# A hybrid decoder trunk: the order of projections, state-space quarters and attentions, and the value products of two heads side by side

## The chip, the cores and the metric

The kernel runs on one core of a Trainium2 chip. The metric is the device time of one launch in microseconds (us), as the median of several runs. Everything is in 32-bit floats; the large products use pairs of rounded numbers (a high and a low part, type fp32r) so that three fast products stand for one exact one.

## The reference

The input is one sequence of 512 tokens with 1024 features. Two layers follow. Layer 0 mixes tokens in two ways side by side: half of the features go through a diagonal state-space model (32 groups of 16 channels with 64 complex states), the other half through "stick-breaking" attention (8 heads of 64). Layer 1 is a convolution module. After each mixer come a residual, a layer norm, a feed-forward layer with squared ReLU, and again a residual and a layer norm. The part that matters here:

```python
h = x @ mix_w_in[i] + mix_b_in[i]
u, q, k, v = jnp.split(h, [512, 1024, 1536], axis=-1)
s5_out = s5_mixer(u, ...)             # states, gelu, then a gated linear unit (glu)
# attention, per head, strictly causal:
z = einsum(q, k) * scale
log_beta = log_sigmoid(z)
log_keep = where(strict, log_sigmoid(-z), 0.0)
after = cumsum(log_keep, reverse=True) - log_keep
weights = where(strict, exp(log_beta + after), 0.0)
out = einsum(weights, v)
mix = concatenate([s5_out, sb_out]) @ mix_w_out[i] + mix_b_out[i]
```

## The kernel before

Features lie on the 128 partitions and the 512 tokens along the free dimension. Before the change's place the input is transposed and the first projection `u` is made. Then layer 0's mixer runs as a list of steps, `ORDER`, for four quarters of the features (two heads of attention, or a quarter of the state-space groups, each):

- `q0` to `q3` (function `qkv`): three projections, each 24 products of 512 columns through `in_proj` and `gemm` (L206). The result stays in a PSUM bank of the tag `mm` (three banks) until it is copied into `qh`, `ql`, `kh`, `kl` (one buffer each) or `v` (two buffers).
- `s0` to `s3` (`s5_states`): VectorE (DVE) prepares Gx and Cx, TensorE (PE) makes gp, tp, vR and vI, and DVE runs a chain of products and two scans that ends in Sx. Gx, Cx, Tx and Sx have one buffer each, so a quarter's step waits for the outputs of the quarter before.
- `y0` to `y3` (`s5_outputs`): yp, twelve products of 128 columns from Tx, Cx, Sx, then U is updated on DVE.
- `a0` to `a3` (`attention`), described below.
- `gelu`: GELU of all four quarters, with a Tanh on ScalarE (ACT) and a round trip through device memory on the sync engine's (SP's) queue, back into `yf` (tag `wt`, three buffers).
- `glu`: 96 products into `mm` banks, with a Sigmoid for each of four gates.

After the list, `accum` multiplies the state-space half with half of the output matrix (`acmo`, 96 products), and the attention half follows in `tail_norm_lead`.

An attention step has two heads, 0 and 1, which lie on partitions 0 to 63 and 64 to 127. Each head has three groups of score blocks: A (key block 0 against all 512 queries), B (key blocks 1 and 3, 384 and 128 columns), C (key block 2, 256 columns). The string `ATT` lists the order of the groups' steps. `s` is `scores`: products of 64 rows into a bank of the tag `z` (four banks, shared with gp, tp, vR, vI, yp and vt), then Abs, Exp, Ln on ACT, a DVE step, a mask on GpSimd (POOL), and the split into high and low parts; these (`sh`, `sl`) have one buffer for each letter, which both heads share. `w` is `weigh`: products with `tri` and `negs` (constants for the sums over later keys) into the same bank, then Exp into a `wt` buffer (three), a mask on POOL, and, before the change, the value products into the bank `av`, 64 output columns for each head (L685).

The instructions of each engine run in an order that is fixed when the kernel is built: by the order in which the code emits them as far as their inputs and buffers are ready in the builder's plan. The buffers and banks of one tag are handed out in the order of the code. The weights come through `Weights`: raw blocks by DMA on SP's queue, then a high part on ACT (`whi`) and a low part on DVE (`wlo`), two units ahead. `Act` puts a table load on ACT before a function of another set, and ties it behind all functions of the set before: Exp and Ln are one set, Tanh and Sigmoid another. `add_manual_dep` with `NOSYNC` fixes an order on one engine and makes nothing wait.

Of the kernel before, what the change touches and what calls it, by code (L numbers as in the profile page):

```python
# [13 lines left out]
ALU = mybir.AluOpType  # L14
PSUM = bass.MemoryType.PSUM

P = 128
T = 512
# [23 lines left out]
AHEAD = (5, 4)  # L42
FJ = 3
BEFORE = (1, 3, 1, 2)
ATT = "sB0 sC0 wB0 sA0 wC0 sB1 sC1 wB1 sA1 wC1 wA1 wA0"
MIX_BUFS = (3, 4, 1, 4, 3)
WARM = 24
QK_BUFS = (1, 1)
ORDER = "q0 s0 a0 q1 y0 s1 a1 q2 y1 s2 a2 q3 y2 s3 y3 gelu a3 glu".split()


class Weights:
# [56 lines left out]
def units_of(name, w, k0, nk, cols, width):  # L109

    ncol = 1024 // nk
    out = []
    for c in cols:
        base = c // width * width
        src = w[k0 * P : (k0 + nk) * P, base : base + width].rearrange("(k p) n -> p k n", p=P)
        out.append(((name, k0, base), src, nk, ncol, c - base, width))
    return out
# [5 lines left out]
NOSYNC = mybir.DependencyInfo(mybir.DependencyClass.NoSync, mybir.DependencyReason.DATA)  # L123
# [23 lines left out]
def kernel(ctx: ExitStack, tc: tile.TileContext, a: dict, out: bass.AP):  # L147
    nc = tc.nc
    act = Act(tc)
    V, S, G, PE = nc.vector, nc.scalar, nc.gpsimd, nc.tensor  # L150
# [7 lines left out]
    def page(name, dt=F32R):  # L158
        return pgp.tile([P, T], dt, tag="pg", name=name, bufs=24)
# [35 lines left out]
    def split(hi, lo, src):  # L195
        i0 = S.copy(hi, src).ins  # L196
        i1 = V.tensor_sub(lo, src, hi.bitcast(F32)).ins  # L197
        return i0.name, i1.name
# [19 lines left out]
    units = units_of("u", w_in, 0, 8, range(0, 512, 128), 128)  # L218
    for o in ORDER:
        if o[0] == "q":  # L220
# [8 lines left out]
    def psum(tag, name, bufs):  # L229
        return mps.tile([P, T], F32, tag=tag, name=name, bufs=bufs)  # L230
# [4 lines left out]
    def zz(name):  # L235
        return psum("z", name, MIX_BUFS[1])
# [41 lines left out]
    for n in vecs:  # L278
# [3 lines left out]
        while done < m:  # L282
            half, at = divmod(r0 + done, P)
            c = min(m - done, P - at)
# [19 lines left out]
    for j in range(KT):  # L304
        ps = (mm if j % 2 else s5ps)(f"xT{j}")
        for b in range(4):
            ins = PE.transpose(ps[:, b * P : (b + 1) * P], xin[j][:, b, :], ident).ins
# [12 lines left out]
        if j == 2:  # L320
            parp = zz("parp")
            ins = PE.transpose(parp[:, :96], nat, ident[:96, :96]).ins
# [26 lines left out]
    def stt(o, x, s, y, op0, op1):  # L349
        V.scalar_tensor_tensor(o, x, s, y, op0=op0, op1=op1)  # L350
        return o

    def exps(x):
        xc = ts(small(), x, -87.0, 88.0, ALU.max, ALU.min)
        k = ts(small(), xc, LOG2E, MAGIC, ALU.mult, ALU.add)
        ts(k, k, MAGIC, None, ALU.subtract, ALU.bypass)
        r = stt(small(), k, -LN2HI, xc, ALU.mult, ALU.add)
        stt(r, k, -LN2LO, r, ALU.mult, ALU.add)
        s = ts(small(), r, 1.0 / math.factorial(8), None, ALU.mult, ALU.bypass)
        for n in range(7, 0, -1):  # L360
            stt(s, s, 1.0 / math.factorial(n), r, ALU.add, ALU.mult)
        ki = ts(small(16, I32), k, 127.0, 8388608.0, ALU.add, ALU.mult)
        p2 = ki.bitcast(F32)
        e = stt(small(), s, 1.0, p2, ALU.add, ALU.mult)
        m = tt(small(), s, p2, ALU.mult)
        em1 = stt(small(), p2, -1.0, m, ALU.add, ALU.add)
        return e, em1

    ts(LR, LR, -1e-4, None, ALU.min, ALU.bypass)
    dt, _ = exps(LDT)  # L370
# [50 lines left out]
    for k in (2, 3, 4):  # L421
        h = 1 if k < 4 else 2
# [202 lines left out]
    def attention(p, q_, k_, v_):  # L625
        vps = zz(f"vt{p}")
        for b in range(4):
            PE.transpose(vps[:, b * P : (b + 1) * P], v_[:, b * P : (b + 1) * P], ident)
        vt = att.tile([P, 4, P], F32, tag="vt", name=f"vt{p}")
        S.copy(vt, vps.rearrange("p (b c) -> p b c", b=4))  # L630
        av = psum("av", f"av{p}", MIX_BUFS[2])

        groups = {}
        for h in range(2):
            groups[f"A{h}"] = ((h, 0, 0),)
            groups[f"B{h}"] = ((h, 1, 0), (h, 3, 384))
            groups[f"C{h}"] = ((h, 2, 0),)
        at = {(h, kb): (g, o) for g, bl in groups.items() for h, kb, o in bl}
        diag = {"A": slice(0, 1), "B": slice(0, 4, 3), "C": slice(0, 1)}
        zs, sps, summed = {}, {}, [0, 0]  # L640

        def mask(x, g):
            x = x.rearrange("p (b c) -> p b c", c=P)[:, diag[g[0]], :]
            G.affine_select(x, x, pattern=[[0, x.shape[1]], [1, P]], compare_op=ALU.is_gt, fill=0.0,
                            base=0, channel_multiplier=-1)

        def scores(g):
            z = zs[g] = zz(f"z{p}{g}")
            for h, kb, o in groups[g]:
                R = slice(64 * h, 64 * h + 64)  # L650
                for i, (u, v) in enumerate(((0, 0), (0, 1), (1, 0))):
                    ins = PE.matmul(z[:, o : o + T - P * kb], k_[u][R, P * kb : P * kb + P], q_[v][R, P * kb :],
                                    start=o == 0 and i == 0, stop=i == 2, skip_group_check=True).ins
                    if o or i:
                        tc.add_manual_dep(ins, opened, NOSYNC, reason="the bank's first product")
                    opened = ins.name
            n = H if g[0] == "C" else T
            z = z[:, :n]
            sp = att.tile([P, T], F32, tag="spt", name=f"sp{p}{g}", bufs=MIX_BUFS[3])[:, :n]
            act(sp, z, AF.Abs)  # L660
            act(sp, sp, AF.Exp, scale=-1.0)
            act(sp, sp, AF.Ln, bias=1.0)
            stt(sp, z, 0.0, sp, ALU.max, ALU.add)
            mask(sp, g)
            hi = att.tile([P, n], F32R, tag=f"sh{g[0]}", name=f"sh{p}{g}", bufs=1)
            lo = att.tile([P, n], F32R, tag=f"sl{g[0]}", name=f"sl{p}{g}", bufs=1)
            split(hi, lo, sp)
            sps[g] = (hi, lo)

        def weigh(g):  # L670
            for h, kb, o in groups[g]:
                for k2 in range(3, kb - 1, -1):
                    g2, o2 = at[h, k2]
                    n = T - P * k2
                    for i in range(2):
                        PE.matmul(zs[g][:, o + P * (k2 - kb) : o + P * (k2 - kb) + n], tri if k2 == kb else negs,
                                  sps[g2][i][:, o2 : o2 + n], start=False, stop=k2 == kb and i == 1, skip_group_check=True)
            n = H if g[0] == "C" else T
            w_ = att.tile([P, T], F32, tag="wt", name=f"w{p}{g}", bufs=MIX_BUFS[4])[:, :n]
            act(w_, zs[g][:, :n], AF.Exp)  # L680
            mask(w_, g)
            for h, kb, o in groups[g]:
                R = slice(64 * h, 64 * h + 64)
                summed[h] += 1
                PE.matmul(av[R, P * kb :], vt[:, kb, R], w_[:, o : o + T - P * kb], start=summed[h] == 1,  # L685
                          stop=summed[h] == 4, skip_group_check=True)

        for x in ATT.split():
            (scores if x[0] == "s" else weigh)(x[1:])
        ch, cl = page(f"ch{p}"), page(f"cl{p}")  # L690
        split(ch, cl, av)
        cat[4 + p] = (ch, cl)
# [40 lines left out]
    hq = {}  # L733
    for o in ORDER:
        if o[0] == "q":
            hq[o[1]] = qkv(int(o[1]))
        elif o[0] == "a":
            attention(int(o[1]), *hq[o[1]])
        elif o[0] == "s":
            s5_states(int(o[1]))  # L740
        elif o[0] == "y":
            s5_outputs(int(o[1]))
        elif o == "gelu":
            gelu()
        else:
            glu()
# [210 lines left out]
    for n in ("ln1_g", "ln2_g", "conv_ln_g"):  # L957
        c = PV[:, vrow[n] : vrow[n] + a[n].shape[0] * KT]
# [148 lines left out]
    for bi, nb in enumerate(FFN_BLOCKS[1]):  # L1107
# [3 lines left out]
        if bi < len(FFN_BLOCKS[1]) - 1:  # L1111
            for f in range(2):
                pss = [nps(f"g{bi}{f}{b}") for b in range(4)]
                for k in range(0, nb, 2):
                    wh, wl = W.next()
                    for b in range(4):
                        for kk in range(2):
                            hh, hl = (t_[:, b * P : (b + 1) * P] for t_ in hs[k + kk])
                            for i, (u, v) in enumerate(((hh, wh), (hl, wh), (hh, wl))):
                                PE.matmul(pss[b], u, v[:, kk, :], start=k + kk == 0 and i == 0,  # L1120
                                          stop=k + kk == nb - 1 and i == 2)
# [68 lines left out]
```

## Time and profile before

| | us |
|---|---|
| median of 3 runs | 1278.25 (1272.75 to 1278.43) |
| the profiled execution | 1277.66, its span 1275.9 |
| PE busy | 1212.0 (95% of the span) |
| DVE busy | 778.6 (61%) |
| ACT busy | 564.8 (44%) |
| POOL busy | 109.5 (9%) |
| mean granted TensorE clock | 0.972 of full speed |

PE, DVE, ACT and POOL are the engines TensorE, VectorE, ScalarE and GpSimd; PEld is PE's loading of weights. A row of a timeline gives the start and the length of one or several merged instructions, the engine, the line of the code, what is written and what it is read from (buffer numbers and the head's number are left out: z1B is block B of attention 1, of either head), and in brackets the idle time just before and what ended it. The ends of PE's products are modelled, so prices are taken from start to start. A 32-bit float product that isn't fp32r shows as two records. The attentions' value products run from 83 to 98 us (attention 0), 128 to 145, 175 to 193, and 239 to 254.

### The profile page before, as it was taken

What the parts mean: (1) busy time and instruction counts of PE and PEld (TensorE: products, weight loads), DVE (VectorE), ACT (ScalarE), POOL (GpSimd) and SP (SyncE); (2) the same over time, 40 slices, a digit from 0 to 9 for tenths busy, and PEclk for the clock granted to TensorE, in tenths of its full rate; (3) what the DMA queues carried; (4) which work ended last, traced back from release to release, by engine and by line L of the source; (5) the groups of instructions that cost most, each with busy time, mean ns of one, the idle gap of its engine ahead of it and who ended that gap; (6) DMA issues with size and microseconds to landing.
All of it is one profiled execution on the core that took longest, in us unless ns stands there. A gap on an engine that the chain in (4) does not pass through costs nothing.

```text
span 1275.9 us, 16671 instructions
## 1 busy us (share of the span) xinstructions
PE 1212.0 (95%) x6559; PEld 1026.5 (80%) x6559; DVE 778.6 (61%) x1321; ACT 564.8 (44%) x1019; POOL 109.5 (9%) x145
## 2 busy tenths in 40 slices
PE   8799998799999999999999999789899999999997
PEld 7677766578988888888899888788898888888886
DVE  6967467357853443433448999999873343444436
ACT  5855364633541422422425675796463241322230
POOL 1011120103000000000031001114310000000000
PEclk9999888899999999999999999979999999999999
DMA  7511101234243233333302320003143232323211
GB/s 186 157 34 50 34 18 43 57 116 133 67 133 98 99 99 99 99 100 99 103 24 78 99 100 1 34 2 100 34 141 111 73 109 79 116 83 116 75 59 66
DMA packets 111662, 105.93 MB, mean 83 GB/s; under 512 B 9378, under 2 KB 99746, under 8 KB 111584
## 3 DMA queue, kind: packets, MB, share of 16 engines
q1 hardware_dynamic: 111424, 104.84, 26.1%
q8 instruction: 51, 0.84, 0.3%
q14 instruction: 27, 0.22, 0.1%
q10 hardware_dynamic: 160, 0.03, 0.0%
HBM read 100.66 MB, written 4.19 MB: 82 GB/s over the span
## 4 chain that ended last, share of the span: by engine, by line
PE 75%; DVE 15%; ACT 3%; issue 3%; DMA 2%; POOL 1%; SPq 1%; DVEq 0%; ACTq 0%; POOLq 0%
PE f L206 22%; PE g L1120 11%; PE acf L206 10%; PE fl L206 4%; PE h L1104 3%; PE tld L206 3%; DVE cz L350 2%; PE tlb L206 2%; PE cv L1019 2%; DVE cy L350 2%; PE acmo L206 2%; DVE wlo L90 2%; PE pl L206 1%; PE pv L206 1%; PE v L206 1%
## 5 line engine op out<-in xcount | busy, mean ns | idle before, releaser
L90 DVE TENSOR_TENSOR wlo<-raw,whi 128x1024 fp32r<-128x1024 f32 x176 | 220.6, 1257 | 250.4 <-ACT whi L89 236.9
L89 ACT CAST whi<-raw 128x1024 fp32r<-128x1024 f32 x176 | 183.9, 1049 | 414.2 <-PE f L206 111.4
L1120 PE MATMUL g<-whi,hh 128*128 128x512 f32 x208 | 81.5, 392 | 0.0
L1120 PE MATMUL g<-wlo,hh 128*128 128x512 f32 x208 | 81.5, 392 | 0.0
L1120 PE MATMUL g<-whi,hl 128*128 128x512 f32 x208 | 81.4, 391 | 0.0
L206 PE MATMUL f<-xdh,whi 128*128 128x512 f32 x208 | 80.9, 389 | 0.0
L206 PE MATMUL f<-xah,whi 128*128 128x512 f32 x208 | 80.9, 389 | 0.0
L206 PE MATMUL f<-xal,whi 128*128 128x512 f32 x208 | 80.9, 389 | 0.0
L206 PE MATMUL f<-xdh,wlo 128*128 128x512 f32 x208 | 80.9, 389 | 0.0
L206 PE MATMUL f<-xdl,whi 128*128 128x512 f32 x208 | 80.9, 389 | 0.0
L206 PE MATMUL f<-xah,wlo 128*128 128x512 f32 x208 | 80.9, 389 | 0.0
L206 PE MATMUL acf<-hl,whi 128*128 128x512 f32 x192 | 75.2, 392 | 0.0
L206 PE MATMUL acf<-hh,whi 128*128 128x512 f32 x192 | 74.9, 390 | 0.0
L206 PE MATMUL acf<-hh,wlo 128*128 128x512 f32 x192 | 74.7, 389 | 0.0
L196 ACT CAST hh<-fr 128x512 fp32r<-128x512 f32 x64 | 39.7, 621 | 71.4 <-DVE fr L346 71.4
L197 DVE TENSOR_TENSOR hl<-fr,hh 128x512 fp32r<-128x512 f32 x64 | 44.2, 692 | 37.3 <-ACT hh L196 37.2
L350 DVE SCALAR_TENSOR_TENSOR cy<-hp,wdw,cy 128x512 f32<-128x512 f32 (+1 forms) x91 | 60.9, 678 | 0.1
L350 DVE SCALAR_TENSOR_TENSOR cz<-hp,wdw,cz 128x512 f32<-128x512 f32 (+1 forms) x86 | 59.8, 699 | 0.0
L1019 PE MATMUL cv<-hph,dh 128*128 128x256 f32 (+1 forms) x113 | 39.9, 353 | 10.0 <-ACT hph L196 8.3
L346 DVE TENSOR_TENSOR fr<-fr 128x512 f32<-128x512 f32 x64 | 43.8, 685 | 5.4 <-ACT fr L135 5.4
L1120 PEld LDWEIGHTS g<-whi,hl 128*128 128x128 f32 x208 | 39.1, 188 | 8.6
L1120 PEld LDWEIGHTS g<-wlo,hh 128*128 128x128 f32 x208 | 39.1, 188 | 8.6
(684 smaller groups left out, 3202.2 us busy)
## 6 DMA issues: line engine op xcount, KB each, us to landing
raw<-in_ffn_w_dram SPq DMA_DIRECT2D x48, 1024.0 KB, 5.4
raw<-in_ffn_w_dram SPq DMA_DIRECT2D x32, 512.0 KB, 3.6
raw<-in_conv_w_pw_dram SPq DMA_DIRECT2D x12, 1024.0 KB, 5.4
raw<-in_mix_w_in_dram SPq DMA_DIRECT2D x16, 512.0 KB, 3.9
xin<-in_x_dram SPq DMA_DIRECT2D x8, 256.0 KB, 3.8
raw<-in_s_w_glu_dram SPq DMA_DIRECT2D x4, 512.0 KB
raw<-in_mix_w_out_dram SPq DMA_DIRECT2D x4, 512.0 KB
raw<-in_mix_w_out_dram SPq DMA_DIRECT2D x2, 1024.0 KB
```

The lines of the kernel that those rows point to most:

```text
L89: i0 = nc.scalar.copy(hi, raw).ins
L90: i1 = nc.vector.tensor_sub(lo, raw, hi.bitcast(F32)).ins
L196: i0 = S.copy(hi, src).ins
L197: i1 = V.tensor_sub(lo, src, hi.bitcast(F32)).ins
L206: ins = PE.matmul(ps[:, c0:c1], u[:, k, ksl], v[:, c0:c1], start=start and k == 0 and i == 0, stop=stop and k == n - 1 and i == 2).ins
L346: V.tensor_tensor(o, x, y, op=op)
L350: V.scalar_tensor_tensor(o, x, s, y, op0=op0, op1=op1)
L1019: PE.matmul(cps[j][:, c0:c1], u, v[:, t + c0 : t + c1], start=t == 0 and i == 0, stop=t == n - 1 and i == 2)
L1104: PE.matmul(ps, u, v, start=k == 0 and i == 0, stop=k == nk - 1 and i == 2)
L1120: PE.matmul(pss[b], u, v[:, kk, :], start=k + kk == 0 and i == 0, stop=k + kk == nb - 1 and i == 2)
```

## The change

`ORDER` puts each `y` behind its `s`, two quarters of the state-space model ahead of attention 0, `gelu` ahead of attention 2 and `glu` ahead of attention 3. The value products leave `weigh` and become a step of their own, `v`, in `ATT`: for each key block, head 0's product and head 1's one after the other, each tied behind the other head's mask. In `ATT` head 0's blocks are scored in the order C, A, B, and head 1's B directly behind head 0's B.

```diff
-ATT = "sB0 sC0 wB0 sA0 wC0 sB1 sC1 wB1 sA1 wC1 wA1 wA0"
+ATT = "sC0 sA0 sB0 sB1 wC0 wB0 sC1 wB1 vB sA1 wA0 wC1 vC wA1 vA"
...
-ORDER = "q0 s0 a0 q1 y0 s1 a1 q2 y1 s2 a2 q3 y2 s3 y3 gelu a3 glu".split()
+ORDER = "q0 s0 y0 s1 y1 a0 q1 s2 y2 a1 s3 y3 q2 gelu a2 q3 glu a3".split()
...
-            mask(w_, g)
-            for h, kb, o in groups[g]:
-                R = slice(64 * h, 64 * h + 64)
-                summed[h] += 1
-                PE.matmul(av[R, P * kb :], vt[:, kb, R], w_[:, o : o + T - P * kb], start=summed[h] == 1,
-                          stop=summed[h] == 4, skip_group_check=True)
+            ws_[g] = w_, mask(w_, g)
+
+        def values(c):
+
+            for (_, kb, o), _ in zip(groups[c + "0"], groups[c + "1"]):
+                for h in range(2):
+                    R = slice(64 * h, 64 * h + 64)
+                    summed[h] += 1
+                    ins = PE.matmul(av[R, P * kb :], vt[:, kb, R], ws_[f"{c}{h}"][0][:, o : o + T - P * kb],
+                                    start=summed[h] == 1, stop=summed[h] == 4, skip_group_check=True).ins
+                    tc.add_manual_dep(ins, ws_[f"{c}{1 - h}"][1], NOSYNC, reason="both heads together")
 
         for x in ATT.split():
-            (scores if x[0] == "s" else weigh)(x[1:])
+            {"s": scores, "w": weigh, "v": values}[x[0]](x[1:])
```

`mask` now returns the name of its instruction; nothing else changes.

More of the change, by code (lines that the diff above doesn't have):

```diff
@@ L639, in attention @@
         diag = {"A": slice(0, 1), "B": slice(0, 4, 3), "C": slice(0, 1)}
-        zs, sps, summed = {}, {}, [0, 0]
+        zs, sps, ws_, summed = {}, {}, {}, [0, 0]
         def mask(x, g):
             x = x.rearrange("p (b c) -> p b c", c=P)[:, diag[g[0]], :]
-            G.affine_select(x, x, pattern=[[0, x.shape[1]], [1, P]], compare_op=ALU.is_gt, fill=0.0,
-                            base=0, channel_multiplier=-1)
+            return G.affine_select(x, x, pattern=[[0, x.shape[1]], [1, P]], compare_op=ALU.is_gt, fill=0.0,
+                                   base=0, channel_multiplier=-1).ins.name
         def scores(g):
```

## The prediction

> **What bounds the kernel now.** I read the page's first two parts, then the busy time by stretch up to the end of the first output products, then the timelines of TensorE (PE), VectorE (DVE) and ScalarE (ACT) in the stretches that showed idle time. The page first:
>
> ```profile
> span 1275.9 us, 16671 instructions
> ...
> PE 1212.0 (95%) x6559; PEld 1026.5 (80%) x6559; DVE 778.6 (61%) x1321; ACT 564.8 (44%) x1019; POOL 109.5 (9%) x145
> ...
> PE   8799998799999999999999999789899999999997
> ...
> PEclk9999888899999999999999999979999999999999
> ```
> TensorE is the bound over the whole span, and its two weak places lie in the first quarter, which is where the change is. The stretches of that quarter (columns: width, busy time of PE, weight loads, DVE, ACT, POOL, then the granted TensorE clock):
>
> ```profile
> 64.00:98.40 34.40, 32.49 (x157) 23.09 (x152) 21.48 (x36) 19.23 (x39) 5.61 (x13) 0.95 0.11 32
> 98.40:145.60 47.20, 44.28 (x270) 33.35 (x269) 29.81 (x53) 22.36 (x45) 6.95 (x13) 0.93 0.12 34
> 145.60:193.00 47.40, 44.29 (x270) 33.59 (x269) 29.96 (x53) 24.36 (x46) 6.70 (x13) 0.93 0.11 34
> 193.00:232.00 39.00, 26.76 (x192) 23.18 (x191) 28.31 (x51) 19.94 (x35) 0.95 (x3) 0.73 0.26 72
> 232.00:272.00 40.00, 37.94 (x160) 27.32 (x160) 17.98 (x26) 21.43 (x34) 3.10 (x9) 0.96 0.15 49
> 272.00:292.00 20.00, 19.88 (x87) 16.12 (x87) 10.23 (x14) 4.41 (x5) 0.00 (x0) 1.00 0.36 122
> ```
> From 64 to 292 us (the last is where the first half of the output projection, `acmo`, ends) PE is busy 32.49 + 44.28 + 44.29 + 26.76 + 37.94 + 19.88 = 205.6 of 228 us: 22.4 idle. Where the clock is granted at c of full speed I count (1 - c) of the busy time as lost: 0.05 x 32.49 + 0.07 x 44.28 + 0.07 x 44.29 + 0.27 x 26.76 + 0.04 x 37.94 = 1.6 + 3.1 + 3.1 + 7.2 + 1.5 = 16.5. So 38.9 of the 228 us are lost, and 189.1 are work at full clock. Half of the loss, 12.2 + 7.2 = 19.4, lies in 193 to 232. What happens there:
>
> ```profile
> 208.87 0.49 PE L563 MATMUL yp<-U,Tx 128*128 128x128 f32 x2 [1.47 <-ACT Tx L528]
> 209.19 0.60 PE L628 MATMUL vt<-ident,v 128*128 128x128 f32 x4
> ...
> 221.66 0.68 PE L652 MATMUL z3B<-qh,kh 64*128 64x384 f32 x1 [1.21 <-DVE U L350]
> ...
> 229.40 0.48 PE L676 MATMUL z3B<-sh3B,negs 128*128 128x128 f32 x1 [5.89 <-ACT sh3B L196]
> ```
> ```profile
> 224.75 1.28 ACT L137 ACT_TABLE_LOAD   x1
> ```
> ```profile
> 224.00:228.00 4.00, 0.00 (x0) 0.00 (x0) 1.64 (x3) 3.97 (x8) 0.00 (x0) 0.50 0.62 157
> ```
> Attention 3 runs beside `s3`, `y3` and `gelu` and nothing else is left to fill PE: the projections are used up and `glu` waits for `gelu`. The head-1 block of z3B (221.66) waits until U has read yp3, because the four PSUM banks of the tag `z` are handed out in program order and yp3 (208.87) has one of them ahead of vt3 (209.19); then the Exp of the attention stands behind the last Tanh and a table load, and PE idles 5.89 us.
>
> **The change part by part.**
>
> *Value products as neighbours.* The count of instructions is the same. Each value product writes 64 output columns: head 0 on partitions 0 to 63, head 1 on 64 to 127. Price alone, from their starts:
>
> ```profile
> 83.40 1.08 PE L685 MATMUL av<-w0B,vt 128*64 128x384 f32 x4
> 84.31 0.59 PE L685 MATMUL av<-w0C,vt 128*64 128x256 f32 x2
> 84.84 0.38 PE L652 MATMUL z0C<-qh,kl 64*128 64x256 f32 x1
> ...
> 95.31 1.07 PE L685 MATMUL av<-w0A,vt 128*64 128x512 f32 x2
> 96.31 0.50 PE L206 MATMUL k<-x0h,whi 128*128 128x512 f32 x1
> ```
> B takes 84.31 - 83.40 = 0.91, C 84.84 - 84.31 = 0.53, A 96.31 - 95.31 = 1.00: 2.44 us a head, 4.88 an attention, 19.5 in four. Do two products on different output columns run together? The `tp` products (32 output columns each) show it:
>
> ```profile
> 205.26 1.72 PE L521 MATMUL tp<-Cx,Gx 128*32 128x128 f32 x62
> 206.91 0.49 PE L535 MATMUL vI<-U,gt 128*128 128x128 f32 x2
> ```
> ```profile
> L521 PE MATMUL tp<-Cx,Gx x256: 196/246/421, 59.3 to 206.7; 128*32 128x64 f32 x37, 128*32 128x128 f32 x36, 128*32 128x96 f32 x28, 128*32 128x32 f32 x27
> ```
> ```profile
> 64.40 1.16 PE L533 MATMUL vR<-U,gt 128*128 128x128 f32 x8
> 65.40 1.06 PE L535 MATMUL vI<-U,gt 128*128 128x128 f32 x8
> ```
> Eight records of 128 columns take 65.40 - 64.40 = 1.00 us, 0.125 each. A quarter's 64 records of `tp` average 80 columns, so alone they would take 64 x 0.125 x 80/128 = 5.0 us; they took 206.91 - 205.26 = 1.65. Four column groups run side by side at a third of the sum. Two groups then give at best half of 19.5 = 9.8 us; the other end is 0 (other instructions set between them). I take 8, nearer to the `tp` row, less a little for pairs that get separated.
>
> The Trainium skill ("TensorE: Matmul & The Clock Gate", "What overlaps and what doesn't") says that matmuls start and end strictly in program order. With two records per product (x4 rows for the two products of B) only head 0's second and head 1's first would overlap: 5/16 of B and a quarter of C and A would go, 1.3 us an attention, 5.4 in four, an estimate by that rule; the sum would come out 2.6 us later. The `tp` rows speak against it.
>
> *Score blocks.* Row groups (64 of 128 rows) already overlap between heads where blocks meet in the queue; before, that is A of head 0 with B of head 1:
>
> ```profile
> 68.15 0.39 PE L652 MATMUL z0A<-qh,kh 64*128 64x512 f32 x1
> 68.36 0.44 PE L652 MATMUL z0B<-qh,kh 64*128 64x384 f32 x1
> ```
> After, it is B with B. A and B of a head have 1,536 columns each, so the overlap is worth the same; and as yp keeps one of four banks in attentions 0 to 2, head 1's B comes late there. Between -1 and +1 us; I take 0. The first weighing now waits for the third block processed (B of head 0 comes after C and A), not the first: one Exp-Ln-mask round later, but the same four blocks are processed before PE goes on with head 1; covered by projection work, cost 0, and 1 to 2 us per attention if that cover is gone (the 6 us stall below holds it).
>
> *Order of quarters.* `y` moves directly behind its `s`, and `s0 y0 s1 y1` ahead of attention 0. Two sides. The loss: attention 0's banks come behind yp1 in program order. By the following rows, it is 14.5 us from the end of one quarter's yp (106.01 + 0.61 = 106.62) to the end of the next quarter's Sx (119.88 + 1.28 = 121.16), and the attention ends 23.7 us after Sx (143.78 + 1.07 = 144.85).
>
> ```profile
> 106.01 0.61 PE L565 MATMUL yp<-Sx,Cx 128*128 128x128 f32 x4
> ...
> 108.91 1.16 PE L533 MATMUL vR<-U,gt 128*128 128x128 f32 x8
> ```
> ```profile
> 74.06 1.28 DVE L346 TENSOR_TENSOR Sx<-m,n 128x508 f32<-128x508 f32 x2
> ...
> 119.88 1.28 DVE L346 TENSOR_TENSOR Sx<-m,n 128x508 f32<-128x508 f32 x2
> ```
> ```profile
> 143.78 1.07 PE L685 MATMUL av<-w1A,vt 128*64 128x512 f32 x2
> ```
> So: Sx0 ends at 75.3, yp0 (2.7 us) at 78, Sx1 at 93, attention 0 at about 117, against 98 before. But y0, s1, y1 are then done, which before stood only at 154. PE has until 117: the rest of s0, y0, s1 and y1 (12), q1 (three projections of 5.46, row below), a first one of q2, and attention 0 (17 by difference: 189.1 less nine projections of 5.46, less 96 products each for glu and acmo at 5.46/24, less about 27 for the quarters, over four), together about 51 of 53 us. The cover is thin: the projections are held by three `mm` banks, since qh and kh have one buffer, so k2 and v2 cannot start before attention 0 has read q0 and k0. I charge 3.5 us more than the 3.5 lost before in 64 to 98 (1.9 idle + 1.6 clock).
>
> ```profile
> 98.48 5.46 PE v L206 x24
> ```
> *Attentions 1 and 2.* s2 and y2 now stand before attention 1 and s3, y3, q2 before attention 2, with a next projection to fill. Each window holds as much as 98 to 145 (43 us of work, less 2 for the pairs), so each keeps that row's loss, 2.9 + 3.1 = 6.0 us: a short wait in the fixed order, and then half clock:
>
> ```profile
> 124.00:128.00 4.00, 2.57 (x16) 1.93 (x14) 3.09 (x7) 2.36 (x6) 1.95 (x3) 1.00 0.45 131
> 128.00:132.00 4.00, 3.78 (x10) 1.90 (x11) 2.51 (x6) 0.48 (x2) 1.02 (x3) 0.63 0.00 0
> 132.00:136.00 4.00, 4.00 (x14) 3.61 (x15) 1.99 (x4) 3.02 (x6) 0.00 (x0) 0.51 0.00 2
> ```
> *gelu before attention 2, glu before attention 3.* `Act` ties each table load behind all functions of the set before. So attention 2's Exps wait for the Tanh of quarter 3, hence for y3: the wait of 221 to 229 moves from attention 3 to 2, where q3 (16.4 us) can fill. Attention 3's Exps wait for glu's four sigmoids, hence for most of glu's 96 products (96/24 x 5.46 = 21.8 us), with one table load more, 1.28 us. Behind that, attention 3 has 21.8 us of acmo beside it. So the 19.4 us in 193 to 232 shrink to a window's usual 6.0. The DMAs that gelu issues on the sync engine's (SP's) queue wait for the same Tanh, and raw weights stand behind them:
>
> ```profile
> SPq L707 <- DVE g L350: 19.3, 2, 17.5
> ```
> In this row they wait 17.5 us and nothing urgent is behind; after, q3's or glu's raws can be. Bounds 0 and 17.5; I take 3, since raws are fetched two units ahead. yf0 to yf3 also go through the three `wt` buffers ahead of attention 2's weights: it needs those only some 5 us after its scores; 0.
>
> *The end.* acmo's last product comes 189.1 - 8 = 181 us of work after 64, plus losses: 7.0 in the first window, 6.0 each in three others, 3 for gelu's DMAs, 1.5 at the end of the stretch (gaps as in 252 to 272, half of 3.6) = 29.5. That is 64 + 210.6 = 274.6 against 292: 17.4 earlier. Later stages are the same; the weights of the first feed-forward layer need the memory of the attention pool, which is free at the end of attention 3. I find that at about 250, against 254 before, so nothing is lost there: 0, up to 5 if it ends late.
>
> The profiled execution took 1277.66 us (span 1275.9 and 1.8 around it), 0.6 under the median of 1278.25. 1277.66 - 17.4 is 1260; I forecast **1260 us**.
>
> **The rivals.**
> 1. *More of the loss goes* (PE is fed in every window). s and y chains no longer queue behind projections, so chain and fill run together: losses of 3 rather than 6 in three windows, none from DMAs, the full 9.8 for pairs: 17.4 + 9 + 3 + 1.8 = 31 earlier, 1246 us. For it: 189.1 us of work is all that PE has to do. Against: the fixed queue, and 43 of 47 us in 98 to 145 although q2 was there to fill.
> 2. *The idle time only moves.* Attention 2 gets the stretch that attention 3 had: q3 and k3 hold two of the three `mm` banks until attention 2's last scores, so glu cannot fill, and raws wait behind gelu's DMAs. Then the 19.4 stay instead of 6.0, and 3.5 in the first window: gain 8 - 3.5 = 4.5 less 1.28 for the load, some 3: 1274 us. For it: the same tables, the same three banks. Against: q3 is 16.4 us of filler that attention 3 did not have.
> 3. *Slower, by the clock.* Attention 0 starts some 20 us later with little beside it; each wait in the fixed order is followed by half clock (124 to 136). If the mean clock over the work falls to 0.80, 181 us of it take 226, and with 20 idle acmo ends at 310: 18 later, 1296. It decides from 181/c + 20 = 228 + 6.4 on, c below 0.84. Against: 0.73 was reached only in the one stretch without filler.
> 4. *Strict order of the products*, as above: 5.4 instead of 8, 1263 us. Chance about one in five whichever of the others holds.
>
> **How the numbers follow.** Forecast 0.47, rival 1 0.25, rival 2 0.16, rival 3 0.12. 0.5% (6.4 us) is about what a measurement of this kernel can tell from no change: faster means below 1272, slower above 1284.6. Rival 2 falls mostly within; the forecast with its bounds (pairs 0 to 9.8, DMAs 0 to 17.5, end 0 to 5) reaches from 1253 to 1284, mostly faster. Faster 0.72, same 0.16, slower 0.12. The range goes from 1240 (rival 1 with a little more) to 1283.
>
> **What would show it.** Right: `av` records of both heads with starts within 0.1 us in pairs, and some 2.4 to 3 us an attention where 4.9 stood; vt0 at about 86, not 66; the two stretches with granted clock 0.5 around 212 to 232 gone; acmo's end near 275; a 13th table load. Wrong: a stretch with PE idle over 5 us beside attention 0 (64 to 117) or beside attention 2 with Tanh or a raw weight as its releaser; head-0 and head-1 value products one after the other; acmo's end at 290 or later; or an earlier end given back in the waits for raw weights of the first feed-forward layer.

## The result, and the profile after

The changed kernel takes 1245.97 us (median of 4 runs, 1245.25 to 1247.01) against 1276.22 for the kernel before in the same comparison: ratio 0.9766, 95% interval 0.9738 to 0.9794. The gain is 30 us where 18 were forecast. The direction and the place were right, the range held the time, but the size is that of rival 1.

The page of the changed kernel, its first two parts:

```profile
span 1245.2 us, 16675 instructions
...
PE 1199.1 (96%) x6559; PEld 1017.1 (82%) x6559; DVE 778.7 (63%) x1321; ACT 566.9 (46%) x1020; POOL 107.2 (9%) x145
...
PE   8899999999999999999999999789899999999997
...
PEclk9999999999999999999999999889899999999999
```
PE is busy 12.9 us less in a span 30.7 us shorter, and the two weak places of the first quarter are gone: in the first ten slices PE's row has no 7 any more and PEclk's no 8. Next, `acmo` in its summary by tile (columns: products, least, median and longest time, first and last start), first before, then after:

```profile
L206 PE MATMUL acmo<-gh,wlo x32: 388/389/395, 269.9 to 291.5; 128*128 128x512 f32 x32
```
```profile
L206 PE MATMUL acmo<-gh,wlo x32: 387/389/450, 227.4 to 261.4; 128*128 128x512 f32 x32
```
The last product of `acmo` starts 30.1 us earlier. From there to the end of the span the kernel before takes 1275.9 - 291.5 = 984.4 us and the changed one 1245.2 - 261.4 = 983.8. So nothing was given back later, and all of the gain lies ahead of `acmo`'s end. The stretches there, cut at the ends of attentions 0, 1 and 2 (width, busy time of PE, weight loads, DVE, ACT, POOL, then the granted clock, as before):

```profile
64.00:118.60 54.60, 52.18 (x371) 40.01 (x368) 47.69 (x86) 25.17 (x48) 6.67 (x14) 0.97 0.14 39
118.60:151.20 32.60, 32.41 (x231) 24.33 (x231) 25.73 (x47) 21.25 (x41) 4.89 (x13) 1.00 0.06 18
151.20:206.50 55.30, 53.10 (x317) 41.23 (x316) 35.11 (x55) 35.10 (x62) 5.07 (x12) 0.97 0.29 86
206.50:261.60 55.10, 54.37 (x255) 42.09 (x254) 29.97 (x41) 31.66 (x51) 4.07 (x12) 1.00 0.23 77
```
PE idles 2.42, 0.19, 2.20 and 0.73 us: 5.5 in all, where 22.4 stood. By the clock 0.03 x 52.18 + 0.03 x 53.10 = 3.2 us go, where 16.5 did. The loss is 8.7 us; the prediction had 29.5. The rest, 197.6 - 8.7 = 188.9 us, is work; the prediction had 181.

The value products of attention 0 and of attention 2, in PE's timeline (each pair, and the row that follows it):

```profile
111.67 1.87 PE L689 MATMUL av<-w0B,vt 128*64 128x384 f32 x8
113.47 0.33 PE L676 MATMUL z0A<-sh0B,negs 128*128 128x128 f32 x1
...
114.48 1.30 PE L689 MATMUL av<-w0C,vt 128*64 128x256 f32 x4
115.71 0.50 PE L676 MATMUL z0A<-sh0A,tri 128*128 128x512 f32 x1
...
117.03 1.54 PE L689 MATMUL av<-w0A,vt 128*64 128x512 f32 x4
118.50 0.44 PE L513 MATMUL gp<-ident,Gx 128*128 128x128 f32 x2
```
```profile
201.16 1.33 PE L689 MATMUL av<-w2B,vt 128*64 128x384 f32 x8
202.42 0.50 PE L676 MATMUL z2A<-sh2A,tri 128*128 128x512 f32 x1
...
203.77 0.65 PE L689 MATMUL av<-w2C,vt 128*64 128x256 f32 x4
204.35 0.50 PE L206 MATMUL gv<-yl,whi 128*128 128x512 f32 x1
...
205.24 1.29 PE L689 MATMUL av<-w2A,vt 128*64 128x512 f32 x4
206.46 0.50 PE L206 MATMUL gv<-yl,whi 128*128 128x512 f32 x1
```
Both heads' products of a block now stand next to each other (x8 and x4, where x4 and x2 stood). From start to the next row, attention 0 takes 1.80 + 1.23 + 1.47 = 4.50 us and attention 2 takes 1.26 + 0.58 + 1.22 = 3.06; worked out in the same way attention 1 takes 4.11 and attention 3 takes 3.52. That is 15.2 against the 19.5 of products made alone: 4.3 saved, not 8. POOL's timeline shows why attention 0's pairs are the slow ones:

```profile
112.00 0.41 POOL L644 TENSOR_SCALAR_AFFINE_SELECT w0B<-w0B 128x256 f32<-128x256 f32 x1 [3.20 <-ACT w0B L141]
...
114.55 0.54 POOL L644 TENSOR_SCALAR_AFFINE_SELECT w0C<-w0C 128x128 f32<-128x128 f32 x1
117.14 0.29 POOL L644 TENSOR_SCALAR_AFFINE_SELECT w0A<-w0A 128x128 f32<-128x128 f32 x1 [2.06 <-ACT w0A L141]
```
These are the masks of the second head's weights. The one of w0A ends at 117.14 + 0.29 = 117.43, 0.4 us after the A pair started (117.03); with 1.00 for one head's A that makes 118.43, and the pair was over at 118.50. For C it is 114.55 + 0.54 + 0.53 = 115.62 against 115.71, for B 112.00 + 0.41 + 0.91 = 113.32 against 113.47. So a pair ends when the second mask has ended and one head's time has gone by. The tie to the other head's mask is an order in the builder's plan and no wait of the first product: that one starts when its own head is ready, and its neighbour waits inside the pair.

### The profile page after: what moved, and what is told of

Same layout as the page of the kernel before. It is cut to its first block, busy times and chain, and to the rows that moved or that the text cites. A ratio compares the mean times of both kernels' runs of the same rounds, so it can differ in the third digit from the quotient of the medians.

```text
span 1245.2 us, 16675 instructions
## 1 busy us (share of the span) xinstructions
PE 1199.1 (96%) x6559; PEld 1017.1 (82%) x6559; DVE 778.7 (63%) x1321; ACT 566.9 (46%) x1020; POOL 107.2 (9%) x145
## 4 chain that ended last, share of the span: by engine, by line
PE 76%; DVE 14%; ACT 4%; DMA 2%; issue 2%; SPq 1%; POOL 1%; DVEq 0%; ACTq 0%; POOLq 0%
PE f L206 23%; PE g L1125 11%; PE acf L206 11%; PE fl L206 4%; PE tlb L206 3%; PE h L1109 3%; PE tld L206 3%; DVE cz L350 3%; PE cv L1024 2%; DVE cy L350 2%; DVE wlo L90 1%; PE pl L206 1%; PE pv L206 1%; PE pg L206 1%; PE acmo L206 1%
## 5 line engine op out<-in xcount | busy, mean ns | idle before, releaser
L1125 PEld LDWEIGHTS g<-whi,hh 128*128 128x128 f32 x208 | 39.1, 188 | 8.5
```

## The experiments

Idle time and mean clock are those from 64 us to the end of `acmo`; "last start" is that of `acmo`'s last product; all three are of the profiled execution. From that start to the end of the span every kernel took 983 to 985 us, so the differences lie ahead of it. Times are medians, compared with the kernel before on the same chip (medians of 1274.9 to 1276.2).

| kernel | us | ratio, 95% interval | last start | idle | clock |
|---|---|---|---|---|---|
| before | 1276.22 | | 291.5 | 22.2 | 0.91 |
| after | 1245.97 | 0.9766 (0.9738 to 0.9794) | 261.4 | 5.5 | 0.98 |
| e1, new order alone | 1255.32 | 0.9839 (0.9820 to 0.9858) | 270.5 | 11.0 | 0.98 |
| e2, new attention alone | 1268.35 | 0.9948 (0.9929 to 0.9967) | 280.2 | 21.5 | 0.93 |
| e3, late part of the order | 1258.62 | 0.9865 (0.9836 to 0.9893) | 277.3 | 16.3 | 0.92 |
| e4, early part of the order | 1250.38 | 0.9799 (0.9779 to 0.9818) | 265.1 | 9.0 | 0.98 |
| e5, blocks without pairs | 1256.75 | 0.9853 (0.9832 to 0.9873) | 269.3 | 7.3 | 0.98 |
| e6, value products twice | 1253.49 | 0.9828 (0.9813 to 0.9842) | 268.6 | 5.7 | 0.99 |
| e7, `glu` behind attention 3 | 1252.16 | 0.9817 (0.9803 to 0.9832) | 265.9 | 9.7 | 0.98 |
| e8, attention 0 first | 1249.14 | 0.9790 (0.9769 to 0.9811) | 262.2 | 7.5 | 0.97 |
| e9, `q2` early | 1251.38 | 0.9812 (0.9794 to 0.9831) | 266.4 | 8.8 | 0.97 |
| e10, `gelu` behind attention 2 | 1251.26 | 0.9810 (0.9787 to 0.9832) | 264.4 | 9.3 | 0.99 |

Theory: the order is the main thing, because it takes away both the idle stretch beside attention 3 and the short wait with half clock in the windows before it. Rivals: the pairs are the main thing; or only the late part of the order (`gelu` and `glu`) matters.

**The two halves of the change alone (e1, e2).** e1 has the new `ORDER` with the old `ATT` and the old place of the value products; e2 the reverse.

```diff
 # e1, against after
-ATT = "sC0 sA0 sB0 sB1 wC0 wB0 sC1 wB1 vB sA1 wA0 wC1 vC wA1 vA"
+ATT = "sB0 sC0 wB0 sA0 wC0 sB1 sC1 wB1 sA1 wC1 wA1 wA0"
 ... (value products back in weigh)
 # e2, against after
-ORDER = "q0 s0 y0 s1 y1 a0 q1 s2 y2 a1 s3 y3 q2 gelu a2 q3 glu a3".split()
+ORDER = "q0 s0 a0 q1 y0 s1 a1 q2 y1 s2 a2 q3 y2 s3 y3 gelu a3 glu".split()
```


> The new ORDER with the old ATT and the value products inside weigh, as before. Theory 1 (the order of the quarters brings nearly all: every attention now has work beside it, and the value pairs save only the 4 us that their records show): 1276 - 26 = about 1250 us, the stretch with half clock at 212 to 232 gone, granted clock over 0.98. Theory 2 (the pairs and the new order of blocks bring most, since shorter attentions leave fewer waits): 1262 us or more.

> The new ATT with value pairs, and the old ORDER. Theory 1: 4 to 8 us faster than before, 1268 to 1272, and the stretch of attention 3 with PE idle and half clock still there at about 205 to 228. Theory 2: at least 15 us faster, 1261 or less.

So the order is the main thing: alone it gives 1 - 0.9839 = 1.6%, about 20 us; the attention alone 0.5%, about 7 us; the sum is near to the 30 of both. e2's 1268 lies in the range of theory 1; e1's 1255 lies between those of the two theories (1250, and 1262 or more), nearer to the first. Stretches by time, first of e1, then of e2:

```profile
120.00:155.00 35.00, 34.45 (x274) 25.03 (x276) 25.82 (x48) 22.02 (x42) 5.03 (x13) 1.00 0.06 17
...
190.00:230.00 40.00, 37.92 (x163) 26.89 (x161) 17.10 (x23) 20.58 (x34) 2.49 (x8) 1.00 0.20 61
```
```profile
120.00:155.00 35.00, 32.44 (x187) 25.24 (x190) 18.35 (x34) 13.65 (x25) 5.71 (x11) 0.85 0.16 46
...
190.00:230.00 40.00, 25.96 (x195) 22.31 (x193) 29.07 (x52) 21.01 (x39) 3.08 (x6) 0.79 0.24 66
```
With the old order (e2) the stretch 190 to 230 still has PE busy for 25.96 of 40 us at a clock of 0.79, and 120 to 155 runs at 0.85. With the new order and the old attentions (e1) both run at 1.00, with 2.1 us idle from 190 to 230 and 0.6 from 120 to 155. So the half clock that the prediction carried into every window hung on the old order, not on the attentions' form.

**The two halves of the order (e3, e4).** Both have the new attentions. e3 keeps the old order up to `q2` and then takes the rest of the state-space quarters, `gelu` and `glu` forward; e4 has the new first half, `q2` ahead of `s3`, and `gelu` and `glu` near their old places. So they aren't clean halves: in both, the last state-space quarters come earlier than in e2.

```diff
 # against after
-ORDER = "q0 s0 y0 s1 y1 a0 q1 s2 y2 a1 s3 y3 q2 gelu a2 q3 glu a3".split()
+ORDER = "q0 s0 a0 q1 y0 s1 a1 q2 y1 s2 y2 s3 y3 gelu a2 q3 glu a3".split()   # e3
+ORDER = "q0 s0 y0 s1 y1 a0 q1 s2 y2 a1 q2 s3 y3 a2 q3 gelu a3 glu".split()   # e4
```


> The new ATT; ORDER as before up to attention 1, then y1 s2 y2 s3 y3 gelu ahead of attention 2 and glu ahead of attention 3. If feeding attention 3 (the 19.4 us lost in 193 to 232) is the main thing: 1276 - 19 = about 1257, and the waits with half clock at 120 to 136 (attention 1) stay. If it is rather that s and y no longer queue behind projections in every window: 1264 or more.

> The new ATT; each y behind its s and two quarters ahead of attention 0, but gelu stands between q3 and attention 3 and glu behind attention 3 again. If feeding attention 3 is the main thing: 10 to 14 us faster than before, 1262 to 1266, with PE idle some 5 us and half clock beside attention 3. If the free s and y chains are the main thing: about 1250.

Against e2 (1268), e4 gains 18 us and e3 gains 10, where both together gain 22. Each comes near a figure named for it, and for different theories: e3's 1258.6 near the 1257 of feeding attention 3 (the half clock beside attention 1 stays, as expected: 0.50 from 124.4 to 134.5), e4's 1250.4 near the 1250 of the free chains. So both parts bring something, and the late part alone is not the cause: the early part brings most of the gain, even with `gelu` and `glu` near their old places. The stretch that held the idle time, in e4:

```profile
190.00:230.00 40.00, 35.03 (x163) 26.14 (x162) 18.70 (x28) 28.75 (x52) 4.99 (x12) 0.96 0.29 79
```
PE is busy for 35.03 of the 40 us there, against 25.96 in e2: the last yp starts at 172.4 there and at 210.4 in e2, so less is left to wait for. In e3 the outcome of rival 2 can be seen; its windows and PE's timeline there:

```profile
190.00:200.00 10.00, 2.52 (x6) 1.29 (x6) 7.04 (x13) 9.10 (x16) 1.89 (x4) 0.63 0.66 198
200.00:210.00 10.00, 8.94 (x33) 7.24 (x32) 2.81 (x5) 4.08 (x9) 1.46 (x3) 0.67 0.13 40
210.00:220.00 10.00, 9.74 (x39) 7.52 (x40) 3.60 (x7) 5.01 (x11) 1.87 (x5) 0.67 0.00 0
```
```profile
195.44 0.80 PE L206 MATMUL gg<-yh,whi 128*128 128x512 f32 x1 [6.82 <-ACT yh L135]
...
199.50 0.47 PE L676 MATMUL z2C<-sh2B,negs 128*128 128x128 f32 x1 [2.04 <-ACT sh2B L196]
```
The idle stretch has moved to attention 2 (2.52 of 10 us busy), with the Tanh's output yh and then the attention's sh2B as releasers, and 20 us at a clock of 0.67 follow. The projections were used up by then (the last product of `v` starts at 186.96), and `glu` can't start before the Tanh. e3's profiled execution (1262.8) is the slowest of its four runs.

**Where the fill stands (e7, e8, e9, e10).** One move each, against after:

```diff
-ORDER = "q0 s0 y0 s1 y1 a0 q1 s2 y2 a1 s3 y3 q2 gelu a2 q3 glu a3".split()
+ORDER = "q0 s0 y0 s1 y1 a0 q1 s2 y2 a1 s3 y3 q2 gelu a2 q3 a3 glu".split()   # e7
+ORDER = "q0 s0 a0 y0 s1 y1 q1 s2 y2 a1 s3 y3 q2 gelu a2 q3 glu a3".split()   # e8
+ORDER = "q0 s0 y0 s1 y1 a0 q1 s2 y2 a1 q2 s3 y3 gelu a2 q3 glu a3".split()   # e9
+ORDER = "q0 s0 y0 s1 y1 a0 q1 s2 y2 a1 s3 y3 q2 a2 q3 gelu glu a3".split()   # e10
```


> The changed kernel with glu behind attention 3 again (a3 glu). If glu ahead of attention 3 matters (its 21.8 us fill, and acmo can follow): PE idle some 5 to 8 us beside attention 3, 4 to 8 us slower than the changed kernel. If glu fills attention 3 as well from behind, since only the priority differs and the Sigmoids then wait for the Exps: within 2 us.

> The changed kernel with attention 0 ahead of y0 s1 y1 again (q0 s0 a0 y0 s1 y1 q1 s2 ...), so that its banks come ahead of yp0. The prediction charged 3.5 us for starting attention 0 behind yp1. If that late start costs: 2 to 4 us faster than the changed kernel's 1246. If the quarters ahead of attention 0 are what keeps every later window fed (each s and y one attention ahead): 4 us slower or more, 1250 up, with attention 1 waiting for s1 y1 s2 y2 in a row.

> The changed kernel with q2 ahead of s3 y3 (a1 q2 s3 y3 gelu a2), so that the projections of quarter 2 are spent before the Exps of attention 2 wait for gelu's last Tanh. If it is q2 behind y3 that fills that wait: PE idle 5 us or more and half clock beside attention 2, 6 to 12 us slower than the changed kernel (the run with the late part alone lost so there). If q3 and the chains are enough: within 3 us.

> The changed kernel with gelu behind q3 and ahead of glu (a2 q3 gelu glu a3): attention 2's Exps no longer wait for the last Tanh, and one table load goes. If that gate is what is left of the loss in 184 to 200 (1.6 us idle, 1.5 of clock): 2 to 4 us faster than 1246. If glu then comes too late for attention 2's end, since gelu's Tanhs wait for attention 2's Exps and its round trip through memory follows: 3 to 8 us slower, with PE idle ahead of the first gg.

e7, e9 and e10 come out 5 to 6 us slower than after by their medians, and their `acmo` ends 3 to 5 us later; e7's interval lies clear of after's, e9's touches it and e10's overlaps it by 0.0007, though no run of the three (1250.0 to 1253.0) is as fast as the slowest of after's (1247.0). Each has one new hole. Windows of e7, e9 and e10:

```profile
210.00:220.00 10.00, 7.61 (x40) 5.66 (x40) 5.19 (x9) 7.32 (x14) 2.58 (x5) 1.00 0.04 7
```
```profile
180.00:190.00 10.00, 7.09 (x33) 5.51 (x32) 7.11 (x11) 9.61 (x17) 2.56 (x4) 1.00 0.47 142
190.00:200.00 10.00, 8.41 (x34) 6.25 (x34) 2.13 (x4) 3.51 (x8) 0.90 (x2) 0.83 0.43 126
```
```profile
200.00:210.00 10.00, 6.57 (x31) 4.97 (x30) 1.39 (x2) 3.16 (x7) 0.00 (x0) 0.91 0.67 169
```
PE's timeline, again of e7, e9 and e10:

```profile
228.84 0.50 PE L206 MATMUL gv<-yh,whi 128*128 128x512 f32 x1 [1.26 <-ACT sg L141]
```
```profile
188.71 0.33 PE L676 MATMUL z2C<-sh2B,negs 128*128 128x128 f32 x1 [2.36 <-ACT sh2B L196]
```
```profile
207.65 0.50 PE L206 MATMUL gg<-yh,whi 128*128 128x512 f32 x1 [2.69 <-ACT yh L135]
```
e7 loses 2.4 us at 210 to 220, beside attention 3. `glu` is not missing there: part of its products run up to 217, and the next come at 228.84, behind a Sigmoid whose table load (226.10) stands behind the last Exp of attention 3. e9 loses 2.9 us at 180 to 190 and some clock behind it: the last projection product starts at 185.97 (in after at 190.67), the last yp at 173.3 (169.1), so no projection was left beside the end of `gelu`, and PE waits for attention 2's sh2B. In e10 `glu` stands directly behind the Tanh, and PE waits 2.69 us in one piece for yh. The idle times are smaller than had been expected: where 5 us or more had been named, e7 has 3.0 us from 202 to 228 and e9 4.5 us from 180 to 200. By time, e7's 6.2 and e10's 5.3 us lie in the ranges named (4 to 8, 3 to 8), and e9's 5.4 between its two cases (6 to 12, and within 3). So each of the three places in the late part is worth 3 to 6 us, and the three holes have one thing in common: products that could fill (of the projections or of `glu`) are used up or held back where ACT or DVE holds the chain. e8 puts attention 0 ahead of y0 again: 1249.1 with an interval that overlaps after's, and its `acmo` ends only 0.8 us later, in a profiled execution that is the fastest of its four. Neither of its two cases (2 to 4 us faster, 4 or more slower) came. Whether the place of attention 0 matters isn't decided; a cost of attention 0's late start does not show.

**The pairs (e5, e6).** e5 has the new order and the new order of blocks, but the value products are back in `weigh`. e6 makes every set of value products twice, so the attention's output comes out doubled.

```diff
 # e5, against after
-ATT = "sC0 sA0 sB0 sB1 wC0 wB0 sC1 wB1 vB sA1 wA0 wC1 vC wA1 vA"
+ATT = "sC0 sA0 sB0 sB1 wC0 wB0 sC1 wB1 sA1 wA0 wC1 wA1"
 ... (value products back in weigh)
 # e6, against after
-            for (_, kb, o), _ in zip(groups[c + "0"], groups[c + "1"]):
+            for kb, o in [(kb, o) for _ in range(2) for _, kb, o in groups[c + "0"]]:
 ...
-                                    start=summed[h] == 1, stop=summed[h] == 4, skip_group_check=True).ins
+                                    start=summed[h] == 1, stop=summed[h] == 8, skip_group_check=True).ins
```


> The new ORDER and the new order of score blocks and weighings, but each value product behind its own weighing again, so heads are no neighbours. With the order alone the time was 1255.3, with pairs 1246. If the pairs themselves bring that difference (fewer us of PE for the value products): within 3 us of 1255. If the new order of blocks brings it (shorter waits inside an attention): within 3 us of 1246, with the value products still at 19 to 20 us of PE.

> The changed kernel with each set of value products made twice, so that the attention's output is doubled; the second set waits for no mask. If two heads' products run side by side whenever both are ready: a second set of B takes about 0.95 us, of C 0.55, of A 1.0, some 10 us in all, and about 10 us more than the changed kernel where PE is the bound. If products start and end strictly in program order: 1.25, 0.8, 1.5, some 14 us. If they don't overlap: 1.8, 1.06, 2.0, 19.5 us.

e1 to e5 changes only the order of the blocks: 1255.3 and 1256.8, intervals that overlap, nothing to be measured, as the case said that credits the pairs themselves. But e5 is not free of pairs: one of the three in each attention, A of head 0 and C of head 1, still meets. PE's timeline of e5:

```profile
113.24 0.64 PE L685 MATMUL av<-w0A,vt 128*64 128x512 f32 x1
113.24 0.65 PE L685 MATMUL av<-w0C,vt 128*64 128x256 f32 x2
...
114.24 0.39 PE L676 MATMUL z0A<-sl0C,negs 128*128 128x256 f32 x1
```
The two take 114.24 - 113.24 = 1.00 us and not 1.53, and by their starts all of e5's value products take 18.8 us, so after saves 3.6 against e5. e5 to after is 10.8 us by the medians and 8.5 between the two profiled spans (1253.7 and 1245.2), more than the records show. The windows of e5 and after (64 to the end of `acmo`) split it:

```profile
64.00:269.50 205.50, 198.20 (x1152) 148.54 (x1143) 138.65 (x229) 113.49 (x201) 22.64 (x51) 0.98 0.19 57
```
```profile
64.00:261.60 197.60, 192.05 (x1169) 147.66 (x1165) 138.49 (x229) 113.18 (x201) 20.70 (x51) 0.98 0.19 59
```
Idle time falls from 7.3 to 5.5, and PE's busy time from 198.2 to 192.1; their sum is the 7.9 us by which the stretch is shorter, and some of the 10.8 is the spread of e5's runs (1254.2 to 1259.2). Of the 6.1 us of busy time, about 0.9 is clock: at 0.50 to 0.51 PE runs for 9.1 us in e5 (64 to 66.2, 195.9 to 202.8) and for 7.2 us in after (64 to 67.8, 194.0 to 197.4). The 1.6 us beyond that and the value products' 3.6 are not traced to a row.

e6 shows what a pair costs when both heads are ready. In attention 2 of e6:

```profile
207.48 1.08 PE L689 MATMUL av<-w2C,vt 128*64 128x256 f32 x8
208.50 0.50 PE L206 MATMUL gv<-yl,whi 128*128 128x512 f32 x1
...
209.39 2.15 PE L689 MATMUL av<-w2A,vt 128*64 128x512 f32 x8
211.47 0.50 PE L206 MATMUL gv<-yl,whi 128*128 128x512 f32 x1
```
C twice takes 208.50 - 207.48 = 1.02 us, A twice 211.47 - 209.39 = 2.08. That is twice one head's time (2 x 0.53 and 2 x 1.00) for two heads twice: once both heads are ready, they run fully side by side. B twice, at 203.29, takes 2.84 and not 2 x 0.91: the second head's mask ends at 203.78 + 0.43 = 204.21, and 1.82 us later is 206.03, where the pairs are over at 206.13. Rival 4, by which only neighbouring records of different heads overlap, would have four products of two records with three overlaps, five records' time: 5 x 0.265 = 1.33 for C and 5 x 0.50 = 2.50 for A. Attention 2 of the changed kernel says the same of a single pair: C takes 0.58, one head's 0.53 and not 0.80. The Trainium skill ("TensorE: Matmul & The Clock Gate", "What overlaps and what doesn't") says that matmuls start and end strictly in program order; if each record counts as a matmul, these rows of products on different output columns do not agree with it, and the measurement decides. By their starts the value products of e6's four attentions take 6.66 + 6.10 + 5.93 + 5.69 = 24.4 us, 9.2 more than after's 15.2, where the three cases had some 10, 14 and 19.5. The whole run costs only 1253.49 - 1245.97 = 7.5 us more than after, and `acmo` ends 7.2 us later. Most of what is missing is clock, since after has 3.4 us at half clock that e6 hasn't, 1.7 us of loss (first after, then e6):

```profile
194.00:197.40 3.40, 3.40 (x10) 2.65 (x9) 2.70 (x5) 3.40 (x9) 0.29 (x1) 0.51 0.49 154
```
```profile
194.00:197.40 3.40, 2.21 (x11) 1.25 (x9) 1.22 (x1) 2.86 (x6) 1.37 (x2) 1.00 0.30 77
```

## Why the prediction was right, and where its size was off

- **Bound and place: right.** The gain lies between 64 us and the end of `acmo`, nothing behind it changed, and the idle stretch beside attention 3 is gone, as is the half clock at 212 to 232: the clock from 206.5 to the end of `acmo` is 1.00.
- **The losses: mis-sized, 29.5 for 8.7.** The step that failed is "each keeps that row's loss, 2.9 + 3.1 = 6.0 us". It took the wait in 124 to 136 as a property of an attention window. e2 (old order, still 0.85 in 120 to 155) and e1 (1.00) show that it belongs to the old order; that the quarters' chains stood behind projections there is my reading of the code. The windows lost 0.2, 3.8 and 0.7 where 6.0, 6.0 and 7.5 were charged, and the first one 4.0 where 7.0 was; with the 3 us for gelu's DMAs this is 20.8 too much.
- **Attention 0's late start: no charge seen.** 3.5 us of the first window's 7.0 were for it. The parts of the sum were near (vt0 came at 90.80 for "about 86", the end of attention 0 at 118.6 for "about 117"), but the cover held, and e8, which starts it early again, is not faster.
- **The DMAs of gelu: 3 us charged, none seen.** The queue's waits (engine, line, for what, total, times, longest):

```profile
SPq L712 <- DVE g L350: 4.8, 1, 4.8
```
  They wait 4.8 us and not 17.5, and the longest wait of PE in attention 2 has an attention weight as its releaser and no raw weight:

```profile
192.25 0.38 PE L652 MATMUL z2C<-qh,kh 64*128 64x256 f32 x1 [1.19 <-ACT w2C L141]
```
- **The pairs: 8 us charged, 4.3 seen in the records.** The mechanism (side by side, as in `tp`) was right, and e6 shows it at its full half price. What the step left out is the second head's mask, which is late inside the pair: attention 0's pairs take 4.50 - 2.44 = 2.1 us longer than two ready heads need. By time, e5 to after, the pairs gave about as much as the 8 or more (7.9 us ahead of `acmo`'s end, 10.8 by the medians), and why it is more than the records show isn't settled. The two tells that I named did not come: 3.06 to 4.50 us an attention in place of 2.4 to 3, and starts within 0.1 us in one pair alone, C of attention 2, since a late mask doesn't allow them.
- **The work: 181 forecast, 188.9 found.** 3.7 of the difference are the pairs. The other 4 need not be work. e2 and e3 have the same products as after, and busy time times clock gives 194.87 x 0.93 = 181 and 197.24 x 0.92 = 181 for them, but 192.05 x 0.98 = 188 for after (each with about 1 us of rounding in the clock). So this count moves by some 7 us without a product more or less, of which waits inside the pairs make about 1 (value products of 14.2 us in e2, 15.2 in after), and it is low where much of the stretch runs at half clock, as it did in the kernel before. That points to the rule of the sum that counts (1 - c) of the busy time as lost: it puts too much on the clock. Why, and how much of the 16.5 us it is, stays open.
- **The table load: right.** One more, 1.28 us:

```profile
L137 ACT ACT_TABLE_LOAD  x13: 1283/1283/1283, 3.5 to 849.2; - x13
```
- **The rivals.** Rival 1's 1246 is the time that came, and its reason (s and y chains no longer queue behind projections) fits e4, where the early part brings most of the gain. That its number is so near is luck in part: the pairs gave 4.3 by the records and not 9.8, and the losses fell to 8.7 and not to its 17.5, so its work is 9.6 us too low and its losses 8.8 too high. Rival 2 didn't happen here, but the idle time beside attention 2 that it forecast is there in e3 and e9. In both the projections were used up before it; that raw weights wait behind `gelu`'s DMAs was not seen in these rows. Rival 3 did not happen: the mean clock is 0.98, far from its 0.84.

Two errors of opposite sign stand in the forecast: 274.6 - 20.8 + 7.9 = 261.7, where `acmo` ended.

## What to carry to other kernels

Before charging a window's usual loss to a new order, ask what that loss hung on: here it went with the order of steps, and no window kept more than 4.0 us of it. Place steps that only the bounding engine does (projections, a gate's products) beside the chains of the other engines, and count what is left for the last chains: each misplaced one cost 3 to 6 us in e7, e9 and e10. Making products neighbours in a queue isn't enough for them to run side by side; the inputs of the second have to be ready when the first starts.

## What was not expected of the hardware

- Two products on different halves of the output columns take no more time than one, once both are ready (e6: 1.02 and 2.08 us for C and A of two heads, each made twice, where one head alone, made twice, would take 1.06 and 2.00).
- How much idle time is followed by a lower clock isn't settled by these runs. Windows of the changed kernel:

```profile
96.00:100.00 4.00, 3.32 (x25) 2.80 (x24) 3.83 (x9) 1.34 (x4) 1.12 (x3) 1.00 0.00 0
100.00:104.00 4.00, 3.81 (x27) 3.27 (x25) 3.93 (x9) 3.45 (x6) 0.20 (x1) 1.00 0.00 0
188.00:192.00 4.00, 3.06 (x14) 2.20 (x12) 0.75 (x2) 1.76 (x3) 0.00 (x0) 1.00 0.26 76
```
0.68 us idle at 96 to 100 left the clock at 1.00; 0.94 us at 188 to 192 was followed by the 3.4 us of half clock at 194.0 to 197.4 shown above; in the kernel before 1.43 us at 124 to 128 was followed by half clock. These 3.4 us are all that is left of the lower clock between 68 us and the end of `acmo`.
